# Softmax probabilities of two attention groups turned by DMA instead of TensorE

## The chip, the core and the metric

The kernel runs on one NeuronCore of a Trainium2 chip. The metric is device time in microseconds (us) from launch to end, the median of several runs. In the profile PE is TensorE's matmuls, PEld its weight loads, DVE VectorE, ACT ScalarE, POOL GpSimd, and SP the engine whose queue issues all of this kernel's DMAs.

## What is computed

One layer over x of 1024 rows by 1024 columns, in float32. A projection `x @ w_in + b_in` is split among four groups of 256 columns each: A (a gated mixing of 128-row blocks), B (band attention: a chunk of 64 rows sees itself and the 8 chunks before it), C (sparse attention: an indexer's scores pick the 256 best keys of each query) and M (attention into 256 memory rows). Each group's output is multiplied by a gate, the four are joined, projected once more and normalised.

```python
yb = chunk_band_attention(heads(bq), heads(bk), heads(bv), b_rel)      # 4 heads of 64
yc = dsa_attention(heads(cq), heads(ck), heads(cv), iq..., ik, iw, t5_table)
ym = memory_attention(heads(mq), km, vm)                                # 4 heads of 64
mixed = concatenate([ya * silu(a_g), yb * silu(bg), yc * silu(cg), ym * silu(mg)])
y = mixed @ w_out + b_out
return layer_norm(alpha * x + y, ln_g, ln_b)
# each attention:  p = softmax(q @ k.T / 8 + bias);  out = p @ v
```

## The kernel before

Queries are worked in eight row blocks of 128 (`rb`), heads in pairs. One row block of one head pair is an `Item` with four kinds of parts:

- `scores`: six matmuls (three products of the high and low halves of q and k, for each of two heads) into two PSUM banks, a maximum on DVE, the exponential on ACT, which leaves the unnormalised probabilities in float32 in the tile `sc`, queries on the partitions.
- `turn`: the product with v wants keys on the partitions, so TensorE transposes each 128x128 block of `sc` against an identity into a PSUM bank `pt`; `spread` then makes the fp16 high half `ph` on ACT and the fp16 rest `pl = pt - ph` on DVE, both in SBUF.
- `values`: for each block two matmuls, with `ph` and with `pl` as the stationary operand, into the bank `pv` (`pv_mm`); `normalized` divides by the row sum.
- `close`: one more transpose of the result, the product with the gate on DVE (tile `mix`), and a store to DRAM.

A row block of M has 4 such blocks of 128x128 (two heads by 256 memory rows). One of B has 1, 2, 3, 4, 5, 5, 5, 5 key blocks for its eight row blocks, and two heads. One of C has rb + 1 key blocks and two heads. With two pairs in each group this makes 64 blocks for M, 120 for B and 144 for C, 328 in all.

`parts_of` writes the parts of successive items in an interleaved order: scores of item t, then the turn of item t - 1, with the values of t - 1 chunk by chunk, the last values of t - 2 and the close of t - 3. `weave` goes through these parts and after each takes some steps of a filler: one step is three 128x512 matmuls of a projection (`project`) that a later stage needs. `Filler` also holds the search for the 256 best keys (`search`: 31 rounds of counting on ACT and DVE), paced by `PACE`. The constants `LAG` and `LAG_S` say how many parts back a filler step may be pulled forward. The final order on each engine is set by a scheduler from these parts, their priorities and the buffers.

The stages follow each other: M pair 0 and pair 1, B pair 0 and pair 1, then C, at the end woven with the output projection. Weights are loaded by SP into `raw` (two buffers), rounded to a high half on ACT and completed by the rest on POOL (`wblock`, tile `wblk`). The gates that a projection has made are stored to DRAM (`gate_half`) and loaded again by `gate_of`, 512 columns at a time, one load for four row blocks.

Tiles that matter here: `sc` (tag S, four buffers; an item of M takes one, an item of B two), `ph` and `pl` (three buffers each), PSUM banks `qk` (two), `pt` (three), `pv` (one).

Of the kernel before, what the change touches and what calls it, by code (L numbers as in the profile page):

```python
# [24 lines left out]
P = 128  # L25
# [28 lines left out]
WO_V = 2  # L54
LAG, LAG_S = 22, 6
INDEX_ORDER, EARLY = "h0 q2 h1 a0 q3 h2 h3", "a1 m0 m1"
# [6 lines left out]
OUT_FROM, OUT_PER = 3, 1  # L63
S4, EV, WB, SB, BOOST = 8, 4, 5, 4, 400
BANKS = {"pp": 2, "qk": 2, "pt": 3, "pv": 1}

# [9 lines left out]
def tile_trunk(ctx, tc, x, mem, ln_in_g, ln_in_b, w_in, b_in, a_ln_g, a_ln_b, a_ws, a_bs,  # L76
# [112 lines left out]
    def wblock(w, c0, m=P):  # L189

        raw = E.tile([P, KT, P], F32, tag="raw", bufs=2, name="raw")
        loads.append(SP.dma_start(out=raw[:, :, :m], in_=w[:, c0:c0 + m].rearrange("(k p) c -> p k c", p=P)).ins)
        ts = []
        if m < P:
            both = gp.tile([P, 2, 2, KT // 2, m], F32R, tag="planes", bufs=1, name="wnar")
        for q in range(2):
            t = E.tile([P, 2, 4, P], F32R, tag="w", bufs=WB, name="wblk") if m == P else both[:, q]
# [321 lines left out]
    def spread(pt, n):  # L519

        ph = gp.tile([P, 512], F16, tag="ph", bufs=3, name="ph")
        pl = gp.tile([P, 512], F16, tag="pl", bufs=3, name="pl")
        S.activation(ph[:, :n], pt[:, :n], AF.Copy)
        V.tensor_sub(pl[:, :n], pt[:, :n], ph[:, :n])
        return ph, pl

    def pv_mm(pv, j, ph, pl, c, v3, first, last):
        PE.matmul(pv[:, j * 192:j * 192 + 192], ph[:, c:c + P], v3.rearrange("p t d -> p (t d)"),
                  start=first, stop=False)
        PE.matmul(pv[:, j * 192:j * 192 + 128], pl[:, c:c + P], v3[:, 0:2].rearrange("p t d -> p (t d)"),  # L530
                  start=False, stop=last)
# [16 lines left out]

    gates = {}
# [69 lines left out]

    def weave(parts, steps=None, n=0, pacing=()):  # L620

        fillers = [(Filler(steps, (PE,), LAG), n)] if steps else []
        for part in parts:
            part()
            mark()
            for f, n in (*fillers, *pacing):
                f.take(n / len(parts))
        for f, _ in fillers:
            f.finish()

    def mix_of_m(pair, rb, q):
        d = {}

        def scores():
# [12 lines left out]
        def turn():  # L647
            pt = bank("pt")
            for j in range(4):
                PE.transpose(pt[:, j * P:(j + 1) * P], d["sc"][:, j * P:(j + 1) * P], ident)  # L650
            d["p"] = spread(pt, 512)

        def values():
            ph, pl = d["p"]
            pv = bank("pv")
            for odd in range(2):
                for r in range(2):
                    pv_mm(pv, odd, ph, pl, (2 * odd + r) * P, v3m[pair][:, r, odd], r == 0, r == 1)
            d["o"] = normalized(pv, d["rsum"], 6)

        def close():
            t = small([P, P], "mix")
            gated(d["o"], gate_of(6 + pair, rb), t)
            store_mix(6 + pair, rb, t)

        return Item(scores, [turn], [values], close)

    def mix_of(kt, rb, kb0, st, near, far_of, last):

        q, k, v3 = st  # L670
        nk = rb + 1 - kb0
# [5 lines left out]
        def scores():  # L677
# [5 lines left out]
            for a, b in pieces_of(n):  # L683
                accs = [bank("qk") for _ in range(2)]
                two_heads(accs, b - a, q, k, rb * P, kb0 * P + a)
# [23 lines left out]
        def values(odd, c):  # L709
            if not odd and not c:  # L710
                d["pv"] = bank("pv")
            ph, pl = d["p", odd, c]
            for j in range(min(4, nk - c)):
                pv_mm(d["pv"], odd, ph, pl, j * P, v3[:, kb0 + c + j, odd], c + j == 0, c + j == nk - 1)
            if odd and c == chunks[-1]:
# [4 lines left out]

        steps = [(odd, c) for odd in range(2) for c in chunks]
        return [Item(scores, [lambda s=s: turn(*s) for s in steps], [lambda s=s: values(*s) for s in steps], close)]


# [6 lines left out]
    def attention_of_m(pair, q):  # L731
        return parts_of([mix_of_m(pair, rb, q) for rb in range(NB)])

# [144 lines left out]
    def first_filler():  # L878
        yield from gating_of_a(0, 0)
        yield from gating_of_a(0, 1)  # L880
        steps = queries_of_m(1, mq[1])
        for _ in range(KT):
            yield next(steps)
        nat = a_rows(ga[0])
        vts = a_norms(nat, 0)
        yield from steps
        a_mix(vts, 0, 0)
        vts = a_norms(nat, 1)
        yield from gating_of_a(1, 0)
        a_mix(vts, 0, 1)  # L890
        yield from gating_of_a(1, 1)

    def second_filler():
        yield from B[0].piece("q", 0)
        nat = a_rows(ga[1])
        vts = a_norms(nat, 0)
        yield from B[0].piece("q", 1)
        a_mix(vts, 1, 0)
        vts = a_norms(nat, 1)
        B[0].weight("v")  # L900
        B[0].weight("g")
        yield from B[0].piece("v", 0)
        a_mix(vts, 1, 1)
        yield from B[0].all(B0_ORDER)

# [129 lines left out]
    run(steps)  # L1035
    weave(attention_of_m(0, mq[0]), first_filler(), RATES[0], pace(1))
    weave(attention_of_m(1, mq[1]), second_filler(), RATES[1], pace(2))
    nearB = near_bias("B")

    def mixes_of_b(pair):  # L1040
        items = []
        for rb in range(NB):
# [3 lines left out]
            def last(write, rb=rb):  # L1046
                t = small([P, P], "mix")
                write(t)
# [43 lines left out]
    def mixes_of_c0(rb):  # L1092
        def last(write):
            if rb in opened:
                opened[rb](4, write)
            else:
                t = small([P, P], "mix")
                write(t)
# [5 lines left out]
    weave(parts_of([it for rb in C0_FIRST for it in mixes_of_c0(rb)]), C[1].all(C1_ORDER), C1_STEPS)  # L1104
    gates.pop((4, 0), None)

    L = None

    def mixes_of_c1(rb):
# [30 lines left out]
        def column(k, write):  # L1140
            t = small([P, P], "mix")
            write(t)
# [173 lines left out]
```

## Time and profile before

| | before |
|---|---|
| median of 3 runs (lowest to highest) | 701.08 us (699.09 to 703.03) |
| the profiled execution | 701.02 us |
| its span, first to last instruction | 699.1 us |
| mean granted TensorE clock | 0.993 |
| PE busy, share of the span | 660.8 us, 95% |
| DVE | 527.4 us, 75% |
| ACT | 415.7 us, 59% |
| POOL | 259.1 us, 37% |

The busy time of PE counts a matmul from its start to its modelled end, and matmuls overlap, so a busy PE is not one at its peak. How often a new matmul starts is read from the timeline. The stages lie in the span as follows, by the first scores of each: M from 199.9 us, B from 332.3 us, C from 477.2 us, the last close near 663 us, and the rest of the output projection after it.

### The profile page before, as it was taken

Reading aid. Unit: us, or ns where it says so; the run is one execution under the profiler, and the core shown is the slowest. Engines: PE = TensorE matmul, PEld = TensorE weight load, DVE = VectorE, ACT = ScalarE, POOL = GpSimd, SP = SyncE. Lnnn points to the kernel's source line nnn. Section 1 sums busy time; section 2 is a strip of 40 time slices with the busy share of each in tenths; the row PEclk is TensorE's granted clock in tenths of the full one; section 3 lists DMA queues with packets and bytes.
Section 4 is the critical chain, followed back from the end, with each engine's and each line's share of the span. In section 5 each row is a group of like instructions: output and inputs, shape, how many; then the busy total and the mean of one; then the engine's idle time right before and its main releaser. Section 6 shows DMA issues by size and latency. Waiting matters only on the chain. (4 is left out here: it accounts for less than half of the span.)

```text
span 699.1 us, 11217 instructions
## 1 busy us (share of the span) xinstructions
PE 660.8 (95%) x3882; PEld 507.6 (73%) x3882; DVE 527.4 (75%) x1376; ACT 415.7 (59%) x865; POOL 259.1 (37%) x254
## 2 busy tenths in 40 slices
PE   4889999999999998989999999999899998999895
PEld 3767877776777776767777777777678676777685
DVE  6684235556868989897787879999965789698735
ACT  4764345554789697967787789465355554344210
POOL 4672212530624554132110221022222536457752
PEclk9999999999999999999999999999999999999998
DMA  9792510311321232222110312122102473134111
GB/s 271 229 340 77 167 31 7 115 46 32 101 82 48 76 107 61 75 84 54 57 39 11 89 33 58 29 65 84 53 5 72 150 253 102 68 118 166 57 61 60
DMA packets 67444, 63.49 MB, mean 91 GB/s; under 512 B 9232, under 2 KB 55612, under 8 KB 67388
## 3 DMA queue, kind: packets, MB, share of 16 engines
q1 hardware_dynamic: 67388, 62.78, 29.4%
q8 instruction: 30, 0.49, 0.3%
q14 instruction: 26, 0.21, 0.1%
HBM read 46.70 MB, written 17.64 MB: 92 GB/s over the span
## 5 line engine op out<-in xcount | busy, mean ns | idle before, releaser
L91 PE MATMUL acc<-hTh,wblk 128*128 128x512 f32 (+1 forms) x960 | 311.1, 395 | 3.2 <-ACT hTh L91 1.3
L91 PEld LDWEIGHTS acc<-hTh,wblk 128*128 128x128 f32 x960 | 176.8, 188 | 48.4 <-issue 10.5
L91 PE MATMUL acc<-hTl,wblk 128*128 128x512 f32 (+1 forms) x480 | 186.5, 389 | 0.0
L203 POOL TENSOR_TENSOR wblk<-raw,wblk 128x512 fp32r<-128x512 f32 x72 | 99.1, 1380 | 191.0 <-ACT wblk L91 186.5
L91 PEld LDWEIGHTS acc<-hTl,wblk 128*128 128x128 f32 x480 | 90.4, 188 | 17.5 <-issue 1.8
L91 ACT ACTIVATE jka<-score,cand 128x768 int8<-128x768 f32 (+2 forms) x93 | 96.6, 1039 | 8.3 <-DVE cand L91 6.1
L91 ACT ACTIVATE ph<-pt 128x512 f16<-128x512 f32 (+3 forms) x112 | 51.4, 476 | 37.7 <-PE pt L91 34.8
L91 DVE TENSOR_TENSOR pl<-pt,ph 128x512 f16<-128x512 f32 (+3 forms) x112 | 59.4, 540 | 12.7 <-ACT ph L91 12.2
L91 ACT ACTIVATE sc<-sc,nb 128x640 f32<-128x640 f32 (+7 forms) x64 | 46.6, 730 | 37.4 <-DVE nb L91 37.2
L91 DVE SCALAR_TENSOR_TENSOR score<-relu,iw,score 128x384 f32<-128x384 f32 (+5 forms) x42 | 45.1, 1078 | 20.0 <-ACT relu L91 17.4
L91 ACT ACTIVATE wblk<-raw 128x512 fp32r<-128x512 f32 x72 | 44.5, 628 | 23.5 <-PE acc L91 13.4
L91 PE MATMUL pt<-ident,sc 128*128 128x128 f32 x328 | 57.2, 280 | 0.0
L91 PE MATMUL acc<-woh,mh 128*128 128x512 f32 (+1 forms) x144 | 55.7, 387 | 0.0
L91 PE MATMUL acc<-wol,mh 128*128 128x512 f32 (+1 forms) x144 | 54.2, 377 | 0.0
L91 PE MATMUL acc<-woh,ml 128*128 128x512 f32 (+1 forms) x144 | 54.0, 377 | 0.0
L91 ACT ACTIVATE relu<-sc 128x384 f32<-128x384 f32 (+2 forms) x80 | 36.3, 530 | 25.9 <-PE sc L91 25.8
L91 PE MATMUL pv<-v,ph 128*128 128x192 bf16 x264 | 47.0, 249 | 3.2 <-ACT ph L91 2.6
L91 PEld LDWEIGHTS <-ph 128*128 128x128 f16 x328 | 32.1, 98 | 18.9 <-issue 9.9
L91 PEld LDWEIGHTS pt<-ident,sc 128*128 128x128 f32 x328 | 38.5, 142 | 7.3 <-issue 1.9
L91 PE MATMUL pv<-v,pl 128*128 128x128 bf16 x264 | 43.7, 222 | 0.1
L91 PEld LDWEIGHTS <-pl 128*128 128x128 f16 x328 | 31.6, 98 | 12.3 <-DVE pl L91 3.5
L91 DVE TENSOR_SCALAR_CACHE_REDUCE jk<-planes,lo 128x384 bf16<-128x384 uint16 (+2 forms) x48 | 35.7, 744 | 1.0
(206 smaller groups left out, 1255.9 us busy)
## 6 DMA issues: line engine op xcount, KB each, us to landing
raw<-in_w_in SPq DMA_DIRECT2D x32, 512.0 KB, 3.9
xt<-in_x SPq DMA_DIRECT2D x8, 512.0 KB, 8.6
h_dram<-xt SPq DMA_DIRECT2D x8, 512.0 KB, 5.8
gate<-t SPq DMA_DIRECT2D x16, 256.0 KB, 2.1
rawo<-in_w_out SPq DMA_DIRECT2D x8, 512.0 KB, 4.7
hr<-h_dram SPq DMA_DIRECT2D x8, 512.0 KB, 6.2
out<-hr SPq DMA_DIRECT2D x7, 512.0 KB, 2.7
gate<-gate SPq DMA_DIRECT2D x13, 256.0 KB, 2.7
```

Source lines behind the costliest of these rows:

```text
L91: ins = op(*a, **k)
L203: G.tensor_sub(t[:, 1], r, f32(t[:, 0]))
```

## The change

In M and B the `turn` part goes. Right behind the exponential, `turned` splits the probabilities on POOL, in SBUF and before they are turned: a cast to fp16 (`high`) and a subtraction (`rest`), both written into the unused half of the same `sc` tile (where 4n fp16 columns don't fit into it, `rest` goes over the float32 values). SP then issues DMA transposes into a tile `pT` of 10 blocks (tag pT, `TB` = 4 buffers): one for high and rest together up to four key blocks, otherwise two, one for each. `values` takes its stationary blocks from `pT`. M and B items are ordered by `parts_two_behind`: scores of item t, values of item t - 2, close of t - 3. C keeps the turn by TensorE; its `spread` now also writes into a `pT` tile.

With it come: the second bank of the M and B scores is taken from the tag `pt`; a filler in M and B may lag 15 parts instead of 22 (there are fewer parts per item), the search 4 instead of 6; the steps of the fillers of M are put in another order; `gate_of` loads 128 columns for each row block, one load per item, instead of 512 for four; the `mix` tiles have two buffers instead of three; the small weight block of the indexer takes two other tags.

```diff
-LAG, LAG_S = 22, 6
+LAG, LAG_T, LAG_S = 22, 15, 4
+TB = 4
...
     def spread(pt, n):
-        ph = gp.tile([P, 512], F16, tag="ph", bufs=3, name="ph")
-        pl = gp.tile([P, 512], F16, tag="pl", bufs=3, name="pl")
+        t = gp.tile([P, 10, P], F16, tag="pT", bufs=TB, name="pT")
+        ph, pl = [t[:, a:a + 4].rearrange("p j q -> p (j q)") for a in (0, 4)]
         S.activation(ph[:, :n], pt[:, :n], AF.Copy)
         V.tensor_sub(pl[:, :n], pt[:, :n], ph[:, :n])
...
+    def turned(sc, n):
+        row, nb = sc.bitcast(F16), n // P
+        both = 4 * n <= 2048
+        high, rest = row[:, 2 * n:3 * n], row[:, 3 * n:4 * n] if both else row[:, :n]
+        G.tensor_scalar(high, sc[:, :n], 1.0, 0.0, ALU.mult, ALU.add)
+        G.tensor_sub(rest, sc[:, :n], high)
+        t = gp.tile([P, 10, P], F16, tag="pT", bufs=TB, name="pT")
+        if both:
+            SP.dma_start_transpose(out=t[:, :2 * nb, :], in_=row[:, 2 * n:4 * n])
+        else:
+            SP.dma_start_transpose(out=t[:, :nb, :], in_=high)
+            SP.dma_start_transpose(out=t[:, nb:2 * nb, :], in_=rest)
+        return [t[:, j] for j in range(nb)], [t[:, nb + j] for j in range(nb)]
...
     def gate_of(kt, rb):
-        if (kt, rb // 4) not in gates:
-            t = gp.tile([P, 512], F32, tag="gate", bufs=2, name="gate")
-            SP.dma_start(out=t, in_=gate_dram[kt][rb // 4])
-            gates[kt, rb // 4] = t
-        c = (rb % 4) * P
-        return gates[kt, rb // 4][:, c:c + P]
+        t = gp.tile([P, P], F32, tag="gate", bufs=2, name="gate")
+        SP.dma_start(out=t, in_=gate_dram[kt][rb // 4][:, (rb % 4) * P:(rb % 4 + 1) * P])
+        return t
...
+    def parts_two_behind(items):
+        n = len(items)
+        parts = []
+        for t in range(n + 3):
+            now, _, prev2, prev3 = [items[t - d] if 0 <= t - d < n else None for d in range(4)]
+            if now:
+                parts.append(now.scores)
+            if prev2:
+                parts.append(prev2.values[0])
+            if prev3:
+                parts.append(prev3.close)
+            if prev2:
+                parts += prev2.values[1:]
+        return parts
...
     def mix_of_m(pair, rb, q):
-            accs = [bank("qk") for _ in range(2)]
+            accs = [bank(("qk", "pt")[odd], "qk") for odd in range(2)]
...
-        def turn():
-            pt = bank("pt")
-            for j in range(4):
-                PE.transpose(pt[:, j * P:(j + 1) * P], d["sc"][:, j * P:(j + 1) * P], ident)
-            d["p"] = spread(pt, 512)
+            d["p"] = turned(d["sc"], 512)
...
     def mix_of(kt, rb, kb0, st, near, far_of, last):
+        by_dma = kt < 4
...
                 S.activation(sc[:, :n], sc[:, :n], AF.Exp, bias=nb, accum_out=d["rsum"][:, odd:odd + 1])
+                if by_dma:
+                    d["p", odd] = turned(sc, n)
...
-    weave(parts_of(mixes_of_b(0)), B[1].all(B1_ORDER), RATES[2], pace(3))
-    weave(parts_of(mixes_of_b(1)), C[0].all(C0_PROJ), RATES[3], pace(4))
+    weave(parts_two_behind(mixes_of_b(0)), B[1].all(B1_ORDER), RATES[2], pace(3), LAG_T)
+    weave(parts_two_behind(mixes_of_b(1)), C[0].all(C0_PROJ), RATES[3], pace(4), LAG_T)
```

How the instructions then stand on the engines is shown at three places.

On PE in the stage of M, before: the end of the values of one item (`pv`), then three of the four transposes of the next item's probabilities (`pt` from `sc`), the transpose of a result (`pt` from `o`), and projection steps (`acc`).

```order
L91 LDWEIGHTS ph_2565
L91 MATMUL pv_2658<-v3m_595,ph_2565 128x192
L91 LDWEIGHTS pl_2566
L91 MATMUL pv_2658<-v3m_595,pl_2566 128x128
L91 MATMUL pt_2693<-ident_66,sc_2519 128x128 x3
L91 MATMUL pt_2708<-ident_66,o_2536 128x128
L91 MATMUL acc_2885<-hTh0_113,wblk_2877 128x512 x2
```

The same engine and stage in the change:

```order
L92 LDWEIGHTS pT_2159
L92 MATMUL pv_2311<-v3m_596,pT_2159 128x192
L92 LDWEIGHTS pT_2159
L92 MATMUL pv_2311<-v3m_596,pT_2159 128x128
L92 MATMUL pt_2368<-ident_66,o_2248 128x128
L92 MATMUL qk_2379<-km_675,mqh_1986 128x256
L92 MATMUL qk_2378<-km_675,mql_1987 128x256
```

The transposes of `sc` are gone from PE, 184 over the program; the transposes of results stay.

On POOL in the stage of M, in the change (L535 is the cast and L536 the subtraction of `turned`, L204 the rest of a weight block, L233 and L234 two steps of a gelu, L559 the division by the row sum). Before, the same stretch held L204, L233, L234 and L559 of the old numbering alone:

```order
L535 TENSOR_SCALAR sc_2154<-sc_2154 128x512
L535 TENSOR_SCALAR sc_2215<-sc_2215 128x512
L559 TENSOR_TENSOR o_2193<-o_2193,ri_2191 128x128
L536 TENSOR_TENSOR sc_2154<-sc_2154 128x512
L536 TENSOR_TENSOR sc_2215<-sc_2215 128x512
L204 TENSOR_TENSOR wblk_2588<-raw_2583,wblk_2588 128x512
L204 TENSOR_TENSOR wblk_2593<-raw_2591,wblk_2593 128x512
L233 TENSOR_SCALAR t_2326<-t_2326 128x512
L559 TENSOR_TENSOR o_2248<-o_2248,ri_2246 128x128
L234 TENSOR_TENSOR t_2326<-t_2326,xh_2325 128x512
L535 TENSOR_SCALAR sc_2298<-sc_2298 128x512
L536 TENSOR_TENSOR sc_2298<-sc_2298 128x512
```

The splits stand among weight blocks, gelus and divisions, and POOL works in this order: the division of item 0 (`o_2193`) stands ahead of the subtractions of items 2 and 3.

On SP's queue in the stage of B, row blocks 4 to 6 of pair 0, in the change (L541 and L542 are the transposes of the high and of the rest for five key blocks, L569 a gate load, L573 a store, L193 a weight load). Before, only stores, weight loads and every fourth row block a gate load stood here:

```order
L573 DMA mix0_101<-mix_3825 128x128
L569 DMA gate_4042<-gate2_0_89 128x128
L541 DMA_TRANSPOSE pT_3896<-sc_3867 128x5x128
L573 DMA mix1_102<-mix_3936 128x128
L542 DMA_TRANSPOSE pT_3896<-sc_3867 128x5x128
L541 DMA_TRANSPOSE pT_3904<-sc_3868 128x5x128
L542 DMA_TRANSPOSE pT_3904<-sc_3868 128x5x128
L569 DMA gate_4149<-gate2_0_89 128x128
L541 DMA_TRANSPOSE pT_4009<-sc_3980 128x5x128
L542 DMA_TRANSPOSE pT_4009<-sc_3980 128x5x128
```

Four transposes of an item stand on the queue between stores and gate loads, each of which waits for its own engine.

## Rows read from the trace of the kernel before

**Rows 1.** The page's head and its first part: busy time, share of the span and instructions of each engine.

```profile
span 699.1 us, 11217 instructions
PE 660.8 (95%) x3882; PEld 507.6 (73%) x3882; DVE 527.4 (75%) x1376; ACT 415.7 (59%) x865; POOL 259.1 (37%) x254
```

**Rows 2.** The page's second part, the span in 40 equal slices of 17.5 us: busy tenths of PE, the granted clock, and what the DMA engines moved in GB/s.

```profile
PE   4889999999999998989999999999899998999895
...
PEclk9999999999999999999999999999999999999998
...
GB/s 271 229 340 77 167 31 7 115 46 32 101 82 48 76 107 61 75 84 54 57 39 11 89 33 58 29 65 84 53 5 72 150 253 102 68 118 166 57 61 60
```

**Rows 3.** Busy time of each engine in the stages: before M, M, B, C, and what follows (from and to in us, length, then busy us and count of PE, PEld, DVE, ACT, POOL, the granted clock, the DMA share, GB/s).

```profile
0.00:199.90 199.90, 183.94 (x1012) 141.24 (x1012) 119.70 (x195) 110.98 (x204) 77.53 (x71) 1.00 0.42 127
199.90:332.30 132.40, 125.34 (x739) 96.48 (x738) 115.75 (x336) 109.64 (x242) 53.71 (x68) 1.00 0.26 73
332.30:477.20 144.90, 144.90 (x859) 107.96 (x858) 124.95 (x434) 105.73 (x225) 25.21 (x20) 1.00 0.17 47
477.20:640.00 162.80, 157.78 (x1013) 120.70 (x1013) 131.80 (x360) 81.02 (x178) 69.81 (x66) 0.99 0.35 114
640.00:699.10 59.10, 48.82 (x268) 41.23 (x266) 35.18 (x55) 8.29 (x18) 32.88 (x30) 0.94 0.14 53
```

**Rows 4.** Timeline of PE in the stage of B: start, us from the first start to the last end, what, how many.

```profile
403.51 0.61 PE L91 MATMUL pt<-ident,sc 128*128 128x128 f32 x4
403.95 0.27 PE L91 MATMUL pt<-ident,o 128*128 128x128 f32 x1
...
406.44 0.39 PE L91 MATMUL acc<-hTl,wblk 128*128 128x512 f32 x1
406.67 0.62 PE L91 MATMUL acc<-hTh,wblk 128*128 128x512 f32 x2
```

**Rows 5.** The page's costliest groups, the one of the transposes of probabilities: busy us, mean ns of one, idle time before them.

```profile
L91 PE MATMUL pt<-ident,sc 128*128 128x128 f32 x328 | 57.2, 280 | 0.0
```

**Rows 6.** Waits in M and B (199.9 to 477.2 us): who waited for whom, us in total, times, longest.

```profile
PEld L91 <- DVE pl L91: 3.2, 4, 1.8
PE pv L91 <- DVE pl L91: 2.1, 2, 1.4
```

**Rows 7.** Busy time of DVE (first pair of rows, in the third place behind PE and PEld) on the tile `pl`, and of ACT (second pair) on `ph`, in the stages of M and B.

```profile
199.90:332.30 132.40, 9.78 (x60) 5.64 (x60) 10.24 (x15) 1.00 0.26 73
332.30:477.20 144.90, 17.43 (x104) 10.02 (x104) 20.34 (x42) 1.00 0.17 47
...
199.90:332.30 132.40, 8.79 (x16) 1.00 0.26 73
332.30:477.20 144.90, 18.53 (x44) 1.00 0.17 47
```

**Rows 8.** Instructions of POOL on 128x512, grouped by shape: count, busy us, mean ns of one (the weight rest in M and B together is the first).

```profile
L203 POOL TENSOR_TENSOR wblk<-raw,wblk 128x512 fp32r<-128x512 f32 x32 | 41.5, 1298 | 94.5 <-ACT wblk L91 92.5 <-PE qk L91 1.8
L249 POOL TENSOR_TENSOR v<-vr,v 128x512 bf16<-128x512 f32 x4 | 4.7, 1179 | 27.9 <-DVE v L91 27.9
L232 POOL TENSOR_SCALAR t<-t 128x512 f32<-128x512 f32 x4 | 2.5, 621 | 0.6 <-ACT t L91 0.4
L1115 POOL TENSOR_TENSOR ml<-mixt,mh 128x512 fp32r<-128x512 f32 x7 | 11.0, 1567 | 6.4 <-ACT mh L91 6.4
```

**Rows 9.** Instructions of an item's chain from scores to probabilities, grouped by shape: M's maximum and its scaling on DVE, M's exponential on ACT, then B's two score reductions on DVE and its exponential on ACT.

```profile
L91 DVE TENSOR_REDUCE nb<-qk 128x1 f32<-128x256 f32 x32 | 12.2, 417 | 6.7 <-PE qk L91 6.6
L91 DVE TENSOR_SCALAR nb<-nb 128x2 f32<-128x2 f32 x16 | 5.7, 354 | 0.0
L91 ACT ACTIVATE sc<-qk,nb 128x256 f32<-128x256 f32 x32 | 14.9, 473 | 4.7 <-DVE nb L91 4.7
L91 DVE CUSTOM_DVE_ANT_0 sc<-qk,farB 128x384 f32<-128x384 f32 x16 | 8.3, 553 | 1.9 <-PE qk L91 1.8
L91 DVE CUSTOM_DVE_ANT_0 sc<-qk,nearB,mx 128x256 f32<-128x256 f32 x24 | 10.8, 480 | 1.2 <-PE qk L91 1.1
L91 ACT ACTIVATE sc<-sc,nb 128x640 f32<-128x640 f32 x14 | 11.5, 823 | 4.2 <-DVE nb L91 4.2
```

**Rows 10.** DMAs issued: kind, count, KB each, median us from issue to landing.

```profile
raw<-in_w_in SPq DMA_DIRECT2D x32, 512.0 KB, 3.9
xt<-in_x SPq DMA_DIRECT2D x8, 512.0 KB, 8.6
gate<-gate SPq DMA_DIRECT2D x13, 256.0 KB, 2.7
mix<-mix SPq DMA_DIRECT2D x37, 64.0 KB, 1.6
```

**Rows 11.** Waits of SP's queue in M and B: what the head of the queue waited for, us in total, times, longest.

```profile
SPq L192 <- POOL wblk L203: 68.7, 14, 9.0
SPq L560 <- DVE mix L91: 67.5, 11, 10.9
```

**Rows 12.** Busy time around the start of C, columns as in rows 3.

```profile
460.00:480.00 20.00, 19.41 (x140) 14.91 (x139) 19.63 (x46) 10.51 (x21) 6.53 (x4) 1.00 0.34 95
480.00:500.00 20.00, 19.61 (x110) 15.10 (x109) 19.87 (x45) 8.75 (x23) 6.75 (x6) 1.00 0.16 51
```

**Rows 13.** The chain of waits that ended last, its last long piece: start, us, what.

```profile
662.65 28.81 PE acc L91 x172
```

More of the change, by code (lines that the diff above doesn't have):

```diff
@@ L194, in wblock @@
         if m < P:
-            both = gp.tile([P, 2, 2, KT // 2, m], F32R, tag="planes", bufs=1, name="wnar")
+            narrow = [gp.tile([P, 2, KT // 2, m], F32R, tag=tag, bufs=1, name="wnar") for tag in ("planes", "score6")]
         for q in range(2):
-            t = E.tile([P, 2, 4, P], F32R, tag="w", bufs=WB, name="wblk") if m == P else both[:, q]
+            t = E.tile([P, 2, 4, P], F32R, tag="w", bufs=WB, name="wblk") if m == P else narrow[q]
             r = raw[:, 4 * q:4 * q + 4, :m]
@@ L519, in spread, with pv_mm @@
     def spread(pt, n):
-        ph = gp.tile([P, 512], F16, tag="ph", bufs=3, name="ph")
-        pl = gp.tile([P, 512], F16, tag="pl", bufs=3, name="pl")
+        t = gp.tile([P, 10, P], F16, tag="pT", bufs=TB, name="pT")
+        ph, pl = [t[:, a:a + 4].rearrange("p j q -> p (j q)") for a in (0, 4)]
         S.activation(ph[:, :n], pt[:, :n], AF.Copy)
         V.tensor_sub(pl[:, :n], pt[:, :n], ph[:, :n])
-        return ph, pl
-    def pv_mm(pv, j, ph, pl, c, v3, first, last):
-        PE.matmul(pv[:, j * 192:j * 192 + 192], ph[:, c:c + P], v3.rearrange("p t d -> p (t d)"),
+        return [ph[:, j * P:(j + 1) * P] for j in range(n // P)], [pl[:, j * P:(j + 1) * P] for j in range(n // P)]
+    def turned(sc, n):
[11 more added lines that the diff above has]
+        return [t[:, j] for j in range(nb)], [t[:, nb + j] for j in range(nb)]
+    def pv_mm(pv, j, ph, pl, v3, first, last):
+        PE.matmul(pv[:, j * 192:j * 192 + 192], ph, v3.rearrange("p t d -> p (t d)"),
                   start=first, stop=False)
-        PE.matmul(pv[:, j * 192:j * 192 + 128], pl[:, c:c + P], v3[:, 0:2].rearrange("p t d -> p (t d)"),
+        PE.matmul(pv[:, j * 192:j * 192 + 128], pl, v3[:, 0:2].rearrange("p t d -> p (t d)"),
                   start=False, stop=last)
@@ L657, in values @@
                 for r in range(2):
-                    pv_mm(pv, odd, ph, pl, (2 * odd + r) * P, v3m[pair][:, r, odd], r == 0, r == 1)
+                    pv_mm(pv, odd, ph[2 * odd + r], pl[2 * odd + r], v3m[pair][:, r, odd], r == 0, r == 1)
             d["o"] = normalized(pv, d["rsum"], 6)
         def close():
-            t = small([P, P], "mix")
+            t = small([P, P], "mix", 2)
             gated(d["o"], gate_of(6 + pair, rb), t)
             store_mix(6 + pair, rb, t)
-        return Item(scores, [turn], [values], close)
+        return Item(scores, [], [values], close)
     def mix_of(kt, rb, kb0, st, near, far_of, last):
+        by_dma = kt < 4
         q, k, v3 = st
@@ L683, in scores @@
             for a, b in pieces_of(n):
-                accs = [bank("qk") for _ in range(2)]
+                accs = [bank(("qk", "pt")[odd and by_dma], "qk") for odd in range(2)]
                 two_heads(accs, b - a, q, k, rb * P, kb0 * P + a)
@@ L721, in mix_of @@
         steps = [(odd, c) for odd in range(2) for c in chunks]
-        return [Item(scores, [lambda s=s: turn(*s) for s in steps], [lambda s=s: values(*s) for s in steps], close)]
+        return [Item(scores, [] if by_dma else [lambda s=s: turn(*s) for s in steps], [lambda s=s: values(*s) for s in steps], close)]
     def queries_of_m(pair, q):
@@ L731, in attention_of_m @@
     def attention_of_m(pair, q):
-        return parts_of([mix_of_m(pair, rb, q) for rb in range(NB)])
+        return parts_two_behind([mix_of_m(pair, rb, q) for rb in range(NB)])
     atab = s4("atab", F32)
@@ L880, in first_filler @@
         yield from gating_of_a(0, 1)
-        steps = queries_of_m(1, mq[1])
-        for _ in range(KT):
-            yield next(steps)
+        yield from queries_of_m(1, mq[1])
         nat = a_rows(ga[0])
         vts = a_norms(nat, 0)
-        yield from steps
+        yield from gating_of_a(1, 0)
         a_mix(vts, 0, 0)
         vts = a_norms(nat, 1)
-        yield from gating_of_a(1, 0)
+        yield from gating_of_a(1, 1)
         a_mix(vts, 0, 1)
-        yield from gating_of_a(1, 1)
     def second_filler():
         yield from B[0].piece("q", 0)
+        yield from B[0].piece("q", 1)
         nat = a_rows(ga[1])
         vts = a_norms(nat, 0)
-        yield from B[0].piece("q", 1)
-        a_mix(vts, 1, 0)
-        vts = a_norms(nat, 1)
         B[0].weight("v")
@@ L902, in second_filler @@
         yield from B[0].piece("v", 0)
+        a_mix(vts, 1, 0)
+        vts = a_norms(nat, 1)
+        steps = B[0].all(B0_ORDER)
+        for _ in range(KT):
+            yield next(steps)
         a_mix(vts, 1, 1)
-        yield from B[0].all(B0_ORDER)
+        yield from steps
     def junk():
@@ L1046, in last @@
             def last(write, rb=rb):
-                t = small([P, P], "mix")
+                t = small([P, P], "mix", 2)
                 write(t)
@@ L1096, in last @@
             else:
-                t = small([P, P], "mix")
+                t = small([P, P], "mix", 2)
                 write(t)
@@ L1140, in column @@
         def column(k, write):
-            t = small([P, P], "mix")
+            t = small([P, P], "mix", 2)
             write(t)
```

14 lines of the change are left out of this document (6 added, 8 removed).

## The prediction

> **What bounds the kernel now.** I read the page's busy times first, then the slices, the stages, PE's timeline, and the waits. PE is busy for 95% of the span, DVE for 75% [rows 1]; the slices show PE at 9 tenths or more nearly everywhere from the third slice on, at the full granted clock [rows 2]. In the two stages that the change works on, M and B, PE is busy 125.3 us of 132.4 and 144.9 of 144.9 [rows 3]: here the end is set by what PE has to do, not by a wait. A busy time is not yet a cost, so the price of a transpose is read from the timeline: four of them start at 403.51 us and the next matmul at 403.95 us, 0.11 us each [rows 4], where the grouped row's mean of one is 280 ns [rows 5]. The smaller number counts, since matmuls overlap.
>
> **What leaves PE.** M has 64 blocks and B 120, together 184 of the 328. 64 x 0.11 = 7.0 us leave the stage of M and 120 x 0.11 = 13.2 us that of B, 20.2 us in all. In M this is on the path where PE doesn't wait; in B PE has no idle time at all, so all of it is. With `ph` and `pl` go their waits: PE stood 2.1 us for `pl` [rows 6]. The weight loads of `values` stay as many, only their tile is another.
>
> **What leaves DVE and ACT.** `pl` costs DVE 10.2 us in M and 20.3 in B, `ph` costs ACT 8.8 and 18.5 [rows 7]. Both engines are off the path while PE is full; I cost this at nothing, but it is what lets them follow: DVE is busy 115.8 of 132.4 us in M and 125.0 of 144.9 in B [rows 3], and would otherwise have to do the same in 20 us less.
>
> **What POOL gets.** For each 512 columns a cast, 0.62 us by the nearest row of one input, and a subtraction, 1.30 us by the weight rest in these stages, which has the same form; between 1.18 and 1.57 by the other rows [rows 8]. M has 16 items of 512 columns: 16 x 1.92 = 30.7 us, on top of 53.7 in a stage of about 125. B's 120 blocks are 30 times 512 columns: 57.6 us on top of 25.2 [rows 3] in about 132. That fills POOL to two thirds in both; with the dearer subtraction to 71 and 69%. It is hidden by PE's own work as long as each split comes in time, since POOL works in order and the splits stand among weight blocks and divisions.
>
> **What the queue gets.** 64 transposes (16 in M, 48 in B) and 35 more gate loads (48 for 13). The trace of before has no transpose by DMA, so a block of 128x128 fp16 (32 KB) is bounded by other transfers. From below: the fastest slice moved 340 GB/s [rows 2], 0.10 us for a block. From above: a store of 64 KB, two blocks' worth, lands in 1.6 us [rows 10], 0.8 us for a block if nothing overlaps. I take 0.24 us, 3.9 us for the 16 blocks' worth of a weight load [rows 10], the row nearest in use: long transfers, several under way. An item of M moves 8 blocks, 1.9 us; an item of B with five key blocks moves 20, 4.8 us. After the change an item has (132.4 - 7.0) / 16 = 7.8 us in M and (144.9 - 13.2) / 16 = 8.2 us in B. So the transfers are hidden, and stay so up to 0.98 us for a block in M and 0.41 us in B.
>
> **The added wait.** Values now wait for a chain: M, DVE 2 x 0.42 + 0.35, ACT 2 x 0.47, POOL 1.92 [rows 8, 9], and 2.7 us for 256 KB, the size of its transfer [rows 10], 6.8 us. B with five key blocks: DVE 2 x 0.55 + 2 x 0.48, ACT 2 x 0.82 [rows 9], POOL 2 x 2.4, and 2.7, 11.2 us. With the slowest landing of rows 10, 8.6 us, they are 12.7 and 17.1. Two items of cover are 15.6 and 16.4 us. At a stage's or pair's start the cover is shorter: in the change's order 24 projection matmuls at 0.23 us [rows 4], 5.5 us, and 17 short score matmuls stand between the last score and the first value of M's pair 1. So a few values come late: I take 6 us of new waits, 0.75 us for each of the eight items at the four starts; 0 if all are covered, 16 if every one of the 32 items is half a microsecond late. Behind a waiting value on PE's queue stand projections and the next scores, so such a wait is not made up.
>
> **Edits that cost nothing.** Behind a transpose that waits for POOL, SP holds stores, gate loads and weight loads. SP's head already waits 68.7 us for POOL's weight blocks and 67.5 us for `mix` [rows 11] without PE standing. A gate of 64 KB lands in about 1.6 us [rows 10], with two buffers and one item of time; if SP were held longer, DVE's `mix` would wait, then the scores behind it. The same holds for two `mix` buffers. The fillers' new order and lags move projections, no work. C keeps its transposes. The end of the chain, 28.8 us of output projection [rows 13], is untouched and comes earlier as a whole.
>
> **The sum**, against the profiled execution of 701.0 us (span 699.1; the median, 701.08, is the same): 701.0 - 20.2 - 2.1 + 6.0 = 684.7, so **685 us**. Its own bounds: without new waits, and with all of the 7.1 us that PE idles in M [rows 3] given back, 673.7; with 16 us of new waits 694.7.
>
> [...]
>
> **Rivals.**
> 1. *The transposes become the bound (slower).* Place: SP's transfers in B. It decides from 0.41 us for a block. At the upper bound of 0.8 us, B's 240 blocks take 192 us where 131.7 are there, 60 more: 701.0 - 22.3 + 60.3 = 739 us. M's 128 take 102 us and still fit. For it: blocks are written in short pieces, and small transfers cost most per byte here (1.6 us for 64 KB). Against it: the DMA engines are 26 and 17% busy in these stages [rows 3]. [...] 13%.
> 2. *The chain is late at every item (no change, or a little slower).* POOL in order behind a weight block, a transpose behind a store that waits: SP's longest single waits are 9.0 and 10.9 us [rows 11], more than the margin of 16.4 - 11.2. At 0.7 us for each of the 32 items the gain is gone, 701; at 1.1 us it is 714. 18%, half of it on each side of slower.
> 3. *DVE takes over at the start of C (smaller gain).* From 460 to 500 us DVE is busy 39.5 of 40 us with the masks of C [rows 12]. If these, not PE, set when C starts, B's 13.2 us are not passed on: 701.0 - 7.0 - 2.1 = 691.9. Against it: DVE loses 30.5 us just before [rows 7], more than PE. 9%.
>
> That the change doesn't do what it says is out: 184 transposes are gone from PE's order.
>
> **How the numbers follow.** My forecast has 60%, the rivals 13, 18 and 9. About 0.5%, 3.5 us, is what a measurement of this kernel tells from no change, so 697.5 to 704.5 is the same. Faster: the forecast and rival 3, 69%. Same: half of rival 2, 9%. Slower: its other half and rival 1, 22%. The range reaches from 673, just under the best bound, to 714, the far end of rival 2: the forecast, rival 3 and rival 2, of which I leave some out at both ends, and without rival 1 about 83%. The forecast's own range is 674 to 695.
>
> **What would show it.** Right: PE with 184 fewer matmuls and about 20 us less from the first score of M to the first of C; few waits of PE for `pT`; POOL about 88 us busier; landings of transposes of 3 to 5 us. Wrong: PE's weight loads standing for a transpose in B by several us an item (rival 1 if transfers overlap without a gap, rival 2 if the split or the queue came late), or scores of C waiting for masks (rival 3).

## The result and the profile after

The changed kernel takes 690.96 us (689.41 to 692.53), against 701.06 us of the kernel before in the same runs: ratio 0.9856, 95% interval 0.9819 to 0.9893. The profiled execution took 691.69 us, 9.3 less than the one before. Forecast were 685 us and a gain of 16.3, so 7 us of the gain are missing. Every time here is the median of the executions in the faster of a kernel's two states; one execution of 2094 us, of the kernel with two banks below, is left out by that.

The page's head and first part, as [rows 1], and the granted clock in 40 slices, as [rows 2]:

```profile
span 689.9 us, 11106 instructions
...
PE 638.7 (93%) x3698; PEld 491.2 (71%) x3698; DVE 520.5 (75%) x1312; ACT 390.3 (57%) x801; POOL 347.2 (50%) x350
...
PEclk9999999999999999999999899998999999999998
```

PE has 184 matmuls fewer and POOL 88.1 us more, both as forecast. PE is idle for 51.2 us of its span (689.9 - 638.7) where it was idle for 38.3 (699.1 - 660.8): 12.9 us more, where the forecast's 6.0 us of new waits less the 2.1 that leave make 3.9. DVE is the other surprise: `pl` of M and B, 30.5 us [rows 7], is gone, but its busy time fell by 6.9 us only. By these rows the instructions that the change doesn't touch cost some 23.6 us more (seven of the 64 `pl` that left stood behind C's first scores and are not in the 30.5).

The stages M, B, and from C's first scores to the first close of C, columns as in [rows 3], and below them the last of these stretches before the change:

```profile
199.50:321.20 121.70, 112.10 (x667) 86.50 (x666) 106.17 (x301) 94.31 (x212) 82.17 (x101) 0.99 0.46 111
321.20:452.90 131.70, 121.42 (x706) 90.27 (x705) 119.36 (x407) 93.72 (x190) 72.71 (x79) 0.97 0.51 108
452.90:503.30 50.40, 43.21 (x223) 33.10 (x222) 39.11 (x81) 17.35 (x36) 19.77 (x14) 0.90 0.24 61
```

```profile
477.20:511.80 34.60, 31.71 (x197) 24.29 (x197) 31.36 (x82) 16.09 (x37) 8.18 (x8) 1.00 0.21 65
```

M took 132.4 us and now takes 121.7; B took 144.9 and takes 131.7. At C's first scores the kernel is 24.3 us ahead (477.2 against 452.9), but much of this is work put off. PE's projection matmuls (those that read `wblk`) in M and B, before and after, with their count behind PE's busy time:

```profile
199.90:332.30 132.40, 85.95 (x355) 1.00 0.26 73
332.30:477.20 144.90, 96.94 (x366) 1.00 0.17 47
```

```profile
199.50:321.20 121.70, 85.20 (x337) 0.99 0.46 111
321.20:452.90 131.70, 91.25 (x337) 0.97 0.51 108
```

So 47 of them now come behind C's first scores, 10.8 us at the 0.23 us of [rows 4], and some 13.5 us of the lead are won. Nor is B as full as it was: PE is idle for 10.3 of its 131.7 us, where it was never idle. From there to C's first close the lead falls from 24.3 to 8.5 us (511.8 against 503.3): 32 of the projection matmuls put off are done here, 7.4 us, PE is idle for 7.2 us where it was for 2.9, and its clock is 0.90.

The chain of waits that ended last passes through this place, and it passes through DVE (start, us, what):

```profile
439.81 1.34 DVE jk L92
441.22 2.26 DVE planes L92
448.64 1.34 issue
451.33 1.88 DVE score L92
455.89 1.68 DVE planes L92
...
465.38 2.96 DVE planes L92
468.37 2.01 DVE jk L92
470.40 1.16 DVE score L92
...
474.36 2.26 DVE planes L92
476.62 1.22 DVE o L92
478.79 7.37 PE acc L92 x23
```

`planes`, `jk` and `score` are the masks of C, made from the thresholds that the search found. In DVE's order they stand between the small instructions that TensorE needs: `o`, which empties the one PSUM bank `pv` and then divides. PE's timeline shows one such wait (the bracket is the idle time and who ended it):

```profile
472.15 0.28 PE L92 MATMUL qk<-kl,qh 64*128 64x256 f32 x2
477.88 0.48 PE L92 MATMUL pt<-ident,o 128*128 128x128 f32 x1 [5.46 <-DVE o L92]
```

PE's waits from 430 to 490 us (in total, times, longest), and below them from 430 to 500 us before the change:

```profile
PE pt L92 <- DVE o L92: 5.9, 2, 5.5
PE pv L92 <- DVE o L92: 4.8, 2, 3.5
```

```profile
PE pv L91 <- DVE o L91: 0.5, 1, 0.5
```

So 10.7 us of waiting where there was 0.5 (2.8 if the window before reaches to the first close of C, 511.8 us). A wait can also have a second price. The granted clock fell to half of full speed (0.50) in four stretches between M's start and C's first close, each within an idle time of PE or just behind one (the idle times end at 271.0, 381.8, 456.0 and 477.9 us):

```profile
271.60:275.01 3.41, 3.41 (x14) 2.84 (x12) 3.21 (x12) 3.38 (x10) 2.58 (x4) 0.50 0.18 36
380.80:387.63 6.83, 5.88 (x14) 4.62 (x15) 6.29 (x18) 3.90 (x8) 1.16 (x1) 0.50 0.36 83
455.90:459.31 3.41, 3.36 (x17) 2.96 (x18) 3.34 (x3) 0.00 (x0) 0.00 (x0) 0.50 0.41 79
476.40:483.23 6.83, 5.35 (x14) 4.34 (x15) 6.79 (x11) 1.55 (x3) 2.56 (x2) 0.50 0.32 84
```

In the second stretch a new 128x512 matmul of a projection starts every 0.43 us (382.34 to 386.61 us), where it is every 0.23 us at the full clock [rows 4]. PE is busy for 18.0 us of the four, and by the granted 0.50 that is the work of 9.0, an estimate. Before, M and B had no such stretch [rows 3]. Not every wait is followed by one: behind the wait of 3.5 us that ended at 444.0 us the clock stayed full for 12 us (1.00 up to 455.9).

**Where DVE's 23.6 us came from.** Three groups of DVE instructions, first after, then before the change (busy us, mean ns of one, idle before):

```profile
L92 DVE TENSOR_SCALAR_CACHE_REDUCE jk<-planes,cand 128x384 bf16<-128x384 bf16 (+2 forms) x45 | 33.3, 740 | 0.7
L92 DVE TENSOR_TENSOR o<-o,ri 128x128 f32<-128x128 f32 x32 | 20.5, 642 | 0.2
L92 DVE TENSOR_SCALAR cand<-thr 128x6 uint32<-128x6 uint32 x31 | 12.2, 394 | 0.7
```

```profile
L91 DVE TENSOR_SCALAR_CACHE_REDUCE jk<-planes,cand 128x384 bf16<-128x384 bf16 (+2 forms) x45 | 33.2, 737 | 0.7
L91 DVE TENSOR_TENSOR o<-o,ri 128x128 f32<-128x128 f32 x32 | 15.1, 471 | 0.3
L91 DVE TENSOR_SCALAR cand<-thr 128x6 uint32<-128x6 uint32 x31 | 5.8, 189 | 0.4
```

The counting reductions cost the same (740 and 737 ns); the division `o` costs 5.4 us more and `cand`, six numbers for each partition, 6.4. The rest is spread over other groups, none with more than 2.5. The timeline of the changed kernel shows why (L535 is POOL's cast):

```profile
372.87 0.76 POOL L535 TENSOR_SCALAR sc<-sc 128x640 f16<-128x640 f32 x1 [4.98 <-ACT sc L92]
...
373.07 0.58 DVE L92 TENSOR_SCALAR cand<-thr 128x6 uint32<-128x6 uint32 x1
...
378.08 0.17 DVE L92 TENSOR_SCALAR cand<-thr 128x6 uint32<-128x6 uint32 x1
```

The first `cand` began while POOL's instruction ran and ended at 373.65 us, when that one had ended (373.63). The second, with POOL idle, took 0.17 us. Over the whole trace, all 17 `cand` that began inside an instruction of POOL ended 24 to 93 ns after its end (mean 577 ns; 171 ns for those that didn't begin in one), and all 23 such `o` ended 133 to 222 ns after it (783 against 281 ns). The reduction of `pv` takes 546 ns in the one case and 548 in the other. So the division, which has two SBUF inputs, and `cand`, which has one, ran to the end of POOL's instruction; why these two and not the counting reductions, no run here shows.

### The profile page after: what moved, and what is told of

The parts are those of the page before. It is cut to its first block, busy times and chain, and to the rows that moved or that the text cites. A ratio compares the mean times of both kernels' runs of the same rounds, so it can differ in the third digit from the quotient of the medians.

```text
span 689.9 us, 11106 instructions
## 1 busy us (share of the span) xinstructions
PE 638.7 (93%) x3698; PEld 491.2 (71%) x3698; DVE 520.5 (75%) x1312; ACT 390.3 (57%) x801; POOL 347.2 (50%) x350
## 2 busy tenths in 40 slices
DMA packets 121637, 75.30 MB, mean 109 GB/s; under 512 B 58944, under 2 KB 111468, under 8 KB 121580
## 5 line engine op out<-in xcount | busy, mean ns | idle before, releaser
L92 PE MATMUL acc<-hTh,wblk 128*128 128x512 f32 (+1 forms) x960 | 318.0, 401 | 7.1 <-ACT t L92 3.3
L92 PEld LDWEIGHTS acc<-hTh,wblk 128*128 128x128 f32 x960 | 180.5, 192 | 55.3 <-issue 9.4
L204 POOL TENSOR_TENSOR wblk<-raw,wblk 128x512 fp32r<-128x512 f32 x72 | 101.1, 1410 | 94.3 <-ACT wblk L92 92.4
L92 PEld LDWEIGHTS <-pT 128*128 128x128 f16 x656 | 47.2, 99 | 34.2 <-issue 25.8
L92 PE MATMUL pv<-v,pT 128*128 128x192 bf16 (+1 forms) x528 | 53.5, 236 | 6.4 <-DVE o L92 6.0
L536 POOL TENSOR_TENSOR sc<-sc 128x512 f16<-128x512 f32 (+4 forms) x48 | 55.9, 1170 | 1.9
L535 POOL TENSOR_SCALAR sc<-sc 128x512 f16<-128x512 f32 (+4 forms) x48 | 29.7, 622 | 43.7 <-ACT sc L92 43.1
L92 ACT ACTIVATE pT<-pt 128x512 f16<-128x512 f32 (+3 forms) x48 | 22.2, 483 | 35.5 <-PE pt L92 35.3
L1112 POOL TENSOR_TENSOR comb<-score,nearC 128x256 f32<-128x256 f32 x24 | 18.4, 781 | 36.6 <-DVE mx L92 27.0
L92 DVE TENSOR_SCALAR_CACHE_REDUCE jk<-planes,cand 128x384 bf16<-128x384 bf16 (+2 forms) x45 | 33.3, 740 | 0.7
L92 PEld LDWEIGHTS acc<-woh,mh 128*128 128x128 f32 x144 | 27.3, 190 | 5.0 <-issue 1.2
```

Of the source, the lines that this page charges most:

```text
L92: ins = op(*a, **k)
L535: G.tensor_scalar(high, sc[:, :n], 1.0, 0.0, ALU.mult, ALU.add)
L536: G.tensor_sub(rest, sc[:, :n], high)
L1112: G.tensor_add(t, score[rb][:, n - 256:n], nearC[:, 2 * pair + odd, :])
```

## The experiments

Three theories. **Theory 1:** POOL's splits slow DVE, DVE comes late to C's start, and TensorE stands there. **Theory 2:** the masks in DVE's order bind the start of C whether POOL works or not, so what B saves is not passed on (the prediction's rival 3). **Theory 3:** the transposes' transfers slow DVE. Each ratio is to the kernel before, run beside it on the same chip; the runs were on several chips (the kernel before took 699.99 to 702.13 us there, by its medians), so between two of them a difference of ratios says more than one of times. The scheduler orders each of these kernels anew and no run holds the order fixed, so some of a difference may come from the order alone; how much is not shown.

### POOL's work alone

```diff
+    def pool_split(sc, n):
+        high = sc.bitcast(F16)[:, 2 * n:3 * n]
+        G.tensor_scalar(high, sc[:, :n], 1.0, 0.0, ALU.mult, ALU.add)
+        G.tensor_sub(high, sc[:, :n], high)
```

(called behind the exponentials of M and B in the kernel before.)

> The kernel before, with POOL's cast and subtraction added for each item of M and B and their results used by nobody; TensorE turns the probabilities as before, and nothing is left out. POOL gains about 88 us. Theory 1 (POOL's work on SBUF slows DVE's small operations on SBUF while both run): DVE, 527 us before, gains 15 to 25 us of busy time with no instruction added, the counting step cand and the division o go from means of 189 and 307 ns to 350 to 550, and the time rises by 3 to 15 us, to 704 to 716. Theory 2 (the start of C is bound by DVE's masks anyhow, POOL has no part in it): DVE stays within 3 us of 527, the time within 0.5% of 701. Theory 3 (the transposes' own transfers slow DVE, by writing SBUF): the same as theory 2, since there are none here.

Measured: 713.50 us, ratio 1.0171 (1.0124 to 1.0219). The page's busy times:

```profile
PE 663.3 (94%) x3882; PEld 510.4 (72%) x3882; DVE 541.4 (77%) x1376; ACT 415.7 (59%) x865; POOL 346.2 (49%) x350
```

DVE gains 14.0 us with the same 1376 instructions, a little less than expected, and the kernel takes 12 us longer (the profiled execution, 707.70 us, was the fastest of the five). `o` rose from 471 to 513 ns, `cand` from 189 to 237 only, less than the 350 to 550 expected (the 307 and 310 ns in the expectations are not the mean of the division before, which was 471). POOL's work, used by nobody, slows DVE, and the end moves too. Whether it moves by DVE, or because POOL's weight rests and divisions come later and `sc` is held longer, this run doesn't tell. Theory 3 can't explain it: there are no transposes by DMA here.

### The split on ACT and DVE

```diff
-        G.tensor_scalar(high, sc[:, :n], 1.0, 0.0, ALU.mult, ALU.add)
-        G.tensor_sub(rest, sc[:, :n], high)
+        S.activation(high, sc[:, :n], AF.Copy)
+        V.tensor_sub(rest, sc[:, :n], high)
```

> The changed kernel with the same DMA transposes, but the cast on ACT and the subtraction on DVE, so POOL is as little busy as before the change. Theory 1: cand and o fall back to means near 190 and 310 ns; DVE's total stays near 520 us, as about 24 us of slowing go and some 25 us of own subtractions come; the time is 686 to 695 us. Theory 3: cand and o stay at 400 and 520 ns, DVE rises to about 545 us, and the time to 693 to 702. Theory 2 says nothing of the means; DVE with more own work before C makes C start later than in the changed kernel, 692 to 700.

Measured: 703.09 us, ratio 1.0025 (1.0000 to 1.0050). `cand` fell to 273 and `o` to 466 ns with all 64 transposes in place, so theory 3 is out as the main cause; the 84 ns by which `cand` stays above the kernel before, 2.6 us in all, are open. The time lies above what each theory gave: DVE's subtractions cost 752 ns on average, 35.9 us instead of 25, and DVE stands at 539.5 us. Without them it would be 503.6, 17 less than in the changed kernel. DVE's total is 19 us above the changed kernel's, the time 12.

### M alone, B alone, M and half of B

The three kernels set `by_dma` and the order of parts back to TensorE for B, for M, and for B's second pair:

```diff
-        by_dma = kt < 4
+        by_dma = False       # M alone; kt == 2 for M and half of B
...
-    weave(parts_two_behind(mixes_of_b(1)), C[0].all(C0_PROJ), RATES[3], pace(4), LAG_T)
+    weave(parts_of(mixes_of_b(1)), C[0].all(C0_PROJ), RATES[3], pace(4))
```

> The changed kernel with DMA transposes in M alone; B's probabilities turn on TensorE in the order of before. If what B saves is not passed on to C (theories 1 and 2), M's 10.7 us are nearly all of the gain: 689 to 694 us, about as the whole change. If instead every stage passes on its share and the loss at the start of C takes from both alike, M is worth 10.7 of 23.6, that is 4.6 of the 10.1 us: 695 to 698.

Measured: 691.13 us, ratio 0.9845 (0.9801 to 0.9888).

> The changed kernel with DMA transposes in B alone; M's probabilities turn on TensorE in the order of before. If what B saves is not passed on to C (theories 1 and 2), the first scores of C come some 10 us earlier and the last close 0 to 3 us: 698 to 702 us. If each stage passes on its share, 5.5 us: 694 to 697.

Measured: 699.55 us, ratio 0.9962 (0.9940 to 0.9984).

> The changed kernel with DMA transposes in M and in B's first pair; B's second pair, which runs beside the masks of C, turns on TensorE in the order of before. Theory 1 (POOL's splits slow DVE's masks, and DVE then holds TensorE at the start of C): the masks run without splits beside them, the first pair's 60 transposes, 6.6 us, are passed on in part or whole, and the time is 684 to 688 us, 3 to 7 below M alone (691.1). Theory 2 (DVE's schedule binds the start of C whether POOL works or not): nothing that B saves is passed on, 690 to 692 us.

Measured: 690.55 us, ratio 0.9861 (0.9831 to 0.9891). M alone is worth as much as the whole change; B alone 2.6 us; the half of B with no splits beside the masks adds nothing. PE's busy time with M alone (span 688.4 us), and with M and half of B (span 687.1 us):

```profile
PE 649.9 (94%) x3818; PEld 499.0 (72%) x3818; DVE 521.0 (76%) x1360; ACT 406.1 (59%) x849; POOL 288.4 (42%) x286
```

```profile
PE 646.4 (94%) x3758; PEld 494.9 (72%) x3758; DVE 520.9 (76%) x1336; ACT 398.9 (58%) x825; POOL 316.3 (46%) x318
```

PE's idle time is 38.3 us before the change, 38.5 with M alone, 40.7 with half of B and 51.2 with all of it. From M alone to the whole change PE has 11.2 us less to do and is idle for 12.7 us longer: what B's transposes leave free becomes waiting. What B saves is not passed on, as theory 2 has it, and the third kernel speaks against theory 1.

### No subtraction on POOL

```diff
-        G.tensor_sub(rest, sc[:, :n], high)
...
-            SP.dma_start_transpose(out=t[:, :2 * nb, :], in_=row[:, 2 * n:4 * n])
+            for half in (t[:, :nb, :], t[:, nb:2 * nb, :]):
+                SP.dma_start_transpose(out=half, in_=high)
```

> The changed kernel without POOL's subtraction: the rest of the probabilities is left out of the computation, and the fp16 high half is turned a second time in its place, so that the transfers, the matmuls and DVE's instructions stay. POOL loses about 56 us. Theory 1: DVE falls by 10 to 18 us from 520.5, cand and o from 394 and 642 ns to 200 to 300 and 350 to 500, the waits of TensorE for DVE between 440 and 480 us (11.8 us) shrink by half or more, and the time is 681 to 687 us. Theory 2: DVE loses 0 to 3 us, the time is 689 to 692. Theory 3 (the transposes' transfers slow DVE): as theory 2, since they stay.

Measured: 691.83 us, ratio 0.9888 (0.9863 to 0.9913).

```profile
PE 641.2 (93%) x3698; PEld 491.7 (71%) x3698; DVE 508.1 (74%) x1312; ACT 389.7 (56%) x801; POOL 288.4 (42%) x302
```

DVE is 12.4 us below the changed kernel, `cand` at 251 and `o` at 588 ns (350 to 500 were expected): theory 1's cause is there, in about its size. The end doesn't move: theory 1's consequence is not. PE still waits for `o` behind masks, 3.2 us at 446 and 3.9 at 467 us. At C's first close the kernel is 7.6 us ahead of the changed one (495.7 against 503.3), at a close near 612 us level with it. Three waits of 1.2 to 1.3 us between 550 and 612 us, where the changed kernel has one of 1.5, are part of that; the rest stays open.

### The plain mask

```diff
-        V.tensor_scalar(junk()[:, :n], score[rb], v, None, ALU.is_gt, ALU.add, accum_out=left[:, i:i + 1])
...
-        V.scalar_tensor_tensor(score[rb], score[rb], v, eq[:, :n], ALU.is_lt, ALU.add)
+        V.tensor_scalar(score[rb], score[rb], v, None, ALU.is_lt)
```

> The changed kernel with a plain mask: the breaking of ties among equal scores is left out, so that six DVE instructions for each of six row blocks become one; DVE loses 30 to 38 us just ahead of C. If DVE's masks are what keeps B's saving from C (theories 1 and 2 alike), the waits at 440 to 480 us go and the time is 677 to 683 us. If what is lost at the start of C has another cause (the clock, the order of the items), it stays within 688 to 692.

Measured: 685.15 us, ratio 0.9787 (0.9755 to 0.9819).

> The kernel before with the same plain mask, the breaking of ties left out; DVE loses 22 to 28 us ahead of C. TensorE stood there for only 3 to 5 us, so theories 1 and 2 expect 695 to 699 us, and a distance to the changed kernel with a plain mask of 15 to 20 us, near the 20.2 us of the transposes; if the masks were no bound of the changed kernel, the distance stays 10 us.

Measured: 697.74 us, ratio 0.9976 (0.9956 to 0.9995). Here are 440 to 480 us of the changed kernel, and then with the plain mask:

```profile
440.00:460.00 20.00, 14.78 (x91) 11.62 (x90) 19.93 (x39) 5.62 (x11) 7.74 (x6) 0.91 0.52 102
460.00:480.00 20.00, 14.54 (x81) 11.63 (x80) 19.89 (x27) 7.29 (x16) 12.20 (x7) 0.91 0.24 65
```

```profile
440.00:460.00 20.00, 17.72 (x105) 14.09 (x104) 8.38 (x30) 5.68 (x13) 11.03 (x11) 0.91 0.60 125
460.00:480.00 20.00, 20.00 (x110) 14.81 (x109) 9.47 (x25) 7.00 (x16) 5.17 (x5) 1.00 0.28 80
```

DVE goes from full to under half, and PE from 29.3 to 37.7 us of 40. Without the breaking of ties the changed kernel is 5.8 us faster (4.8 by the ratios) and the one before 2.3, and without their ties the change is worth 12.6 us by the medians (13 by the ratios) instead of 10.1. That is less than was expected (677 to 683, and 15 to 20): by this pair the breaking of ties holds some 3 of the 7 us that are missing, not all.

### The masks split, and a second bank

```diff
+    for k, rb in enumerate((6, 7, 5)):
+        mask(k, rb)
...
+    for k, rb in enumerate((4, 3, 2)):
+        c0_parts.insert(16 + 7 * k, lambda k=k, rb=rb: later_mask(3 + k, rb))
```

> The changed kernel with three of the six masks moved: those of row blocks 6, 7 and 5, which the first items of C need, are made first, and those of 4, 3 and 2, which only later items need, go behind scores in the middle of C's first pair, where DVE is busy 55% of the time. Nothing is left out, and some 16 us of DVE work leave the stretch from 430 to 480 us. Theory 2 (the lump of masks in DVE's order ahead of C holds TensorE, POOL or no POOL): the gain is most of what the plain mask gave, 685 to 688 us. If the masks matter by their place in the planner's order alone and others wait in their stead: 690 to 692.

Measured: 687.25 us, ratio 0.9783 (0.9743 to 0.9824), the fastest kernel of this study that leaves nothing out; its interval just touches the changed kernel's.

```profile
440.00:460.00 20.00, 15.48 (x92) 11.93 (x92) 19.93 (x37) 7.81 (x14) 13.29 (x10) 0.91 0.44 98
460.00:480.00 20.00, 19.86 (x107) 14.56 (x106) 10.88 (x35) 7.56 (x19) 7.84 (x6) 1.00 0.40 108
```

The second half of the lump is gone with three masks, the first half stays. As theory 2 has it.

```diff
-            pv = bank("pv")
+            pv = bank(("pv", "pt")[rb % 2], "pv")
```

> The changed kernel with a second PSUM bank for the values of M and B: every other item takes pv from the tag pt, whose banks these stages hardly use. Nothing is left out. TensorE's waits for the one pv bank, which DVE empties by o, were 1.4, 1.1, 0.9, 3.9 and 1.6 us, 8.9 us in all, with some of the half clock behind them. If these waits are what took the place of the transposes: 681 to 686 us. If DVE's amount of work sets the end and the wait only moves to the division behind it (theory 2 in its strict form): 689 to 692.

Measured: 696.49 us, ratio 0.9930 (0.9899 to 0.9960), 5 us worse than the changed kernel; both expectations missed. PE's waits from M's start to 490 us:

```profile
PE pt L92 <- DVE mx L92: 5.9, 3, 2.9
PE qk L92 <- DVE mx L92: 3.3, 3, 2.0
PE pt L92 <- DVE o L92: 3.1, 2, 2.4
```

The waits for `pv` became waits for `mx`, the row maximum: M and B also take their second score bank from `pt`, and now `pv` took banks of it too. DVE was no sooner with any of it.

> The changed kernel with both: the masks of row blocks 4, 3 and 2 moved into C's first pair, and the second bank for the values of M and B. Nothing is left out. If both the lump of masks and the one bank held TensorE, the waits at 440 to 480 us are nearly gone and less half clock follows: 677 to 683 us, below the plain mask's 685. If the rest of what is lost lies in M and in DVE's total: 684 to 688.

Measured: 692.48 us, ratio 0.9854 (0.9813 to 0.9896). The bank costs 5 us here as it did there; missed as well.

> DMA transposes in M alone, as in the kernel M alone (691.1 us), with the masks of row blocks 4, 3 and 2 moved into C's first pair, as in the kernel with split masks (687.3 us). Nothing is left out. Theory 2: with the lump of masks out of the way B's transposes by DMA pay, while M alone, whose TensorE stood for only 2.7 us at the start of C, gains little from the move: 689 to 692 us, 2 to 4 above the kernel with split masks. Rival: B's transposes by DMA pay nothing in either order, and the move of the masks helps M alone as much: 685 to 688 us.

Measured: 692.61 us, ratio 0.9887 (0.9856 to 0.9917). With the masks split, B's transposes by DMA are worth 5.4 us (692.61 to 687.25, intervals apart), more than the 2 to 4 expected; in the planner's order they were worth 0.2 (691.13 to 690.96). This is the pair that tells theory 2 from the view that B's turns can't pay. Of the 5.4 us, 1.5 are M alone becoming slower by the split (691.13 to 692.61, intervals overlapping), which theory 2 doesn't ask for; against M alone in the planner's order 3.9 us are left.

## Why the prediction was right, and where it was wrong

The sign and the range held. That 691 us lies in the forecast's own range is luck: the range reaches to 695 for late transposes, and these came in time. The mechanism held for M. What B saves turned into waits, in B and at the start of C, and the number is that of rival 3 (691.9), to which the prediction gave 9%.

- *What leaves PE, 20.2 us and 2.1 of waits:* held for M, where PE's busy time fell by 10.9 us with M alone and its idle time stayed. In B only the number fits: it is shorter by 13.2 us, as priced, but 11 of its 120 transposes stood behind C's first scores already, 29 projection matmuls, 6.7 us, now stand there too, its score matmuls keep PE busy for 18.5 us instead of 26.1, and against all this PE is idle for 10.3 us.
- *The transposes:* held. The page's issues (count, KB where it has them, median us from issue to landing), and under them the issues of M alone, 8 blocks each:

```profile
gate<-gate SPq DMA_DIRECT2D x48, 64.0 KB, 2.0
...
gate_a<-gate SPq DMA_DIRECT2D x4, 256.0 KB, 2.9
...
pT<-sc SPq DMA_TRANSPOSE x64, 2.6
```

```profile
pT<-sc SPq DMA_TRANSPOSE x16, 3.2
```

Where 3 to 5 us stood, 3.2 us in M and 2.6 over all. With the start of the transfer in it a block of M takes 0.40 us by this median; rival 1 decides from 0.41 if nothing overlaps, and the DMA engines were busy for 51% in B. The 256 KB of M's eight blocks landed in 3.2 us, a plain load of 256 KB (`gate_a`) in 2.9 us. The blocks move in short pieces, as rival 1 says: by the pages' counts 9232 DMA packets were under 512 B before and 58944 are now. The landings of 3.2 and 2.6 us are those of such packets.
- *The added wait, 6.0 us:* too dear where it was looked for. From M's start to C's first scores PE waited for the transposed blocks 3.6 us in three waits, 3.2 of them at the start of M's pair 1, one of the four places named. Rival 2 is out.

```profile
PE pv L92 <- DVE o L92: 6.8, 7, 3.5
PE pv L92 <- DMA pT<-sc: 3.6, 3, 3.2
```

- *What leaves DVE and ACT, costed at nothing:* here it failed. "Both engines are off the path while PE is full": once PE had less to do, it waited for DVE's `o` for 10.7 us from 430 to 490 us. And "it is what lets them follow" took 30.5 us off DVE; it was 6.9, since the splits put POOL's instructions beside DVE's, and POOL's 88 us were weighed only as POOL's own time. This second error is not shown to cost time: with 12.4 us less on DVE the end stayed where it was.
- *Rival 3, set aside because "DVE loses 30.5 us just before, more than PE":* the same mistake. DVE was full with masks at C's start [rows 12]; PE came to it earlier and found it as full as before. The waits of 10.7 us and the half clock beside them (8.7 us of busy PE in the last two stretches, 4.4 lost) are together no shorter than the 13.2 us that were priced for B. Moving three masks brought 3.7 us back (5.1 by the ratios), leaving out the breaking of ties 5.8 (4.8).

That POOL's slowing is a cause of DVE's 23.6 us is shown (added: 14.0 us more; taken away in part: 12.4 less). That it decides the end of the changed kernel is not: taking half of it away left the time as it was. Some of the missing 7 us lies with the waits of 3.2 and 3.1 us at 268 and 379 us and the half clock beside them; no run took these away alone. So the masks are shown to hold about 3 to 5 of the 7 us, and the rest stays open.

## What to carry to other kernels

When work leaves the engine that bounds, look at the next stage for the engine that is already full there, and see whether its order puts the short instructions that the first waits for behind long ones that could come later: here moving three of them brought back about half of what was missing. When work goes to GpSimd on SBUF operands, charge VectorE too: here `cand` and the division took until the GpSimd instruction's end when they met one (577 against 171 ns and 783 against 281), and the counting reductions cost the same (740 ns, and 737 before). A saving can end at the first place where another engine is full, as B's did at C's masks.

## What was not expected of the hardware

- A DVE instruction of 0.17 us on six numbers for each partition took 0.58 us, until POOL's instruction ended; over the trace 577 ns on average for those that began inside one, 171 for the others. The reduction of `pv` in PSUM (546 against 548 ns) and the counting reductions (740, and 737 before) were no slower.
- PE's idle times of 3.1 us (from 378.7 us) and 5.5 us (from 472.4) each went with 6.83 us at half clock, one of 3.2 us (from 267.8) with 3.41 us. Of the 5.88 us that PE was busy in the first of these stretches 2.9 are lost by the granted 0.50, an estimate. So a wait of 3 us cost up to as much again, and the one of 3.5 us that ended at 444.0 us nothing of the kind.
- A DMA transpose of 8 blocks of 128x128 fp16, 256 KB, landed in 3.2 us, plain loads of 256 KB in 2.9 us and of 64 KB in 2.0 us in the same run.
